# Modulation vectors in the latent attention: two blocks of weight rows at a time, with the eight products ordered behind one another

## The chip, the cores and the metric

The kernel runs on one core of one Trainium2 chip. The metric is device time in microseconds (us) of one execution. Before the change the median of three runs is 1400.68 us (1398.75 to 1402.11).

## The reference, cut to what matters

One encoder layer runs on 1024 prompt frames and 64 sample frames. A conditioning vector c (one per stream, so two) gives six modulation vectors of 1024 elements each, and these shift, scale and gate the layer:

```
mod = silu(c) @ w_ada + b_ada                 # w_ada: 1024 x 6144
shift1, scale1, gate1, shift2, scale2, gate2 = split(mod, 6)
h = rms_norm(x, g_norm1) * (1 + scale1) + shift1
proj = h @ w_in                               # split into latent attention and gated linear attention
x = x + gate1 * (concat(attention, gla) @ w_out)
h2 = rms_norm(x, g_norm2) * (1 + scale2) + shift2
x = x + gate2 * (square(relu(h2 @ w_up)) @ w_down)
```

Vectors 2, 4, 3 and 5 (gate1, scale2, shift2, gate2) are first wanted behind the attention. The change touches how these four are computed.

## The kernel before, in words

Work runs in stages: input projection, gated linear attention, latents and query latents, latent attention (in the trace from about 394 to 605 us), output projection, and the feed-forward layer. Inside a stage several Python generators ("streams") are merged by `interleave` (L50): each `yield pe, wait, cond` says how many nanoseconds of TensorE the piece just written is taken to cost, how long the stream wants to wait before it goes on, and a condition that must hold. `interleave` keeps a planned clock and always goes on with the first stream in its list that is ready. That fixes the order in which instructions are written down. The compiler then orders each engine's instructions itself: an instruction written later may go ahead of one that isn't ready, by the compiler's own estimate. `tc.keep_in_program_order(ins)` takes part of that freedom: it puts `ins` behind the instruction of the same engine that was written just before it. It orders the two, and it neither waits for the first to end nor keeps other instructions from going between.

In the latent attention the streams are, in this order: `weights`, `wo_early`, `mods`, `keys_stream`, `queries_stream`, three `worker`s (one head of one tile of queries each) and `out_early`. `mods` (L1174) computes the four vectors one after the other with `mod_vec` (L148), and takes for each one of the four `mm` banks of PSUM, counted in `state["banks"]`; the workers count theirs in the same place.

`mod_vec` sees the 1024 x 1024 weights of a vector as eight blocks of 128 rows by 1024 columns (512 KB each). A block k is loaded by SP into one of three buffers (`raw`, L155) and multiplied on TensorE by four products (L166). Product j takes the 128x32 operand `scT` as stationary matrix and 256 columns of the block as moving one, and writes partitions 32j to 32j+31 of the accumulator: the four use the four column quarters of the array. The trace holds two records for each product, so eight for a block. Three blocks are loaded ahead, and behind block k's products the load of block k+3 is written, which has to wait for block k's buffer. Behind the eighth block ScalarE copies the accumulator (L174), TensorE transposes it (L178) and VectorE adds the bias (L181).

Three facts of the code set the pace. `wait` begins at 3500 where no rows are handed in (`was is None`), as here. Behind the first block it becomes `min(wait, after)`. Each block adds 500 of planned TensorE time. The planned pace of a vector is so 8 times 4.0 us and 1.8 us around it.

Other callers: `shifts` (L395) calls `mod_vec` for vector 0 during the input projection with `after=1500`. `wo_early` (L1138) goes on when the last queries are projected and `mods` is done.

Of the kernel before, what the change touches and what calls it, by code (L numbers as in the profile page):

```python
# [21 lines left out]
KT = D // P  # L22
# [49 lines left out]
def layer(ctx: ExitStack, tc: tile.TileContext, I, O):  # L72
    nc = tc.nc
    ACT, DVE, POOL, PE, SP = nc.scalar, nc.vector, nc.gpsimd, nc.tensor, nc.sync
# [10 lines left out]
    def tp_bank():  # L85
        return psT.tile([P, 512], F32, name="tp")
# [27 lines left out]
    scT = const.tile([P, KT, 32], F32, name="scT")  # L114
# [30 lines left out]
    def mod_rows(m, k):  # L145
        return I["w_ada"][k * P:(k + 1) * P, m * D:(m + 1) * D]

    def mod_vec(m, wpool, tag, mpool, bank, ahead, was=None, after=3500):  # L148

        wait = 3500 if was is None else 1000  # L150
        was = dict(was or {})

        def load(k):
            was[k] = wpool.tile([P, D], F32, name=tag)
            SP.dma_start(was[k], mod_rows(m, k))  # L155

        for k in range(ahead):
            load(k)
        acc = None
        for k in range(KT):  # L160
            yield 0, wait, None
            wait = min(wait, after)
            if acc is None:
                acc = bank()
            for j in range(4):
                mm = PE.matmul(acc[32 * j:32 * j + 32, 0:256], lhsT=scT[:, k, :], rhs=was[k][:, 256 * j:256 * (j + 1)],  # L166
                               start=(k == 0), stop=(k == KT - 1), tile_position=(0, 32 * j))
                if not ahead:
                    tc.keep_in_program_order(mm)
            if k + ahead < KT and ahead:  # L170
                load(k + ahead)
            yield 500, 0, None
        ms = mpool.tile([P, 256], F32, name="lat", bufs=1)
        ACT.copy(ms, acc[:, 0:256])  # L174
        yield 0, 1000, None
        tp = tp_bank()
        for hf in range(2):
            PE.transpose(tp[:, hf * P:(hf + 1) * P], ms[:, hf * P:(hf + 1) * P], ident)  # L178
        src = tp[:, 0:256].rearrange("p (h j r) -> p j h r", h=2, r=32)[:, :, :, 0:2]
        bia = bT[:, 8 * m:8 * m + 8].rearrange("p (j h s) -> p j h s", h=2, s=1).broadcast_to([P, 4, 2, 2])  # L180
        DVE.tensor_tensor(out=modT[:, m].rearrange("p (j h) s -> p j h s", h=2), in0=src, in1=bia, op=ALU.add)  # L181
        if m in (1, 4):
            i, gT = (0, g1T) if m == 1 else (1, g2T)
            DVE.tensor_scalar(out=G12[:, i], in0=modT[:, m], scalar1=1.0, scalar2=None, op0=ALU.add)
            DVE.tensor_tensor(out=G12[:, i], in0=G12[:, i],
                              in1=gT.rearrange("p (k s) -> p k s", s=1).broadcast_to([P, KT, 2]), op=ALU.mult)
        yield 300, 0, None
# [4 lines left out]
    rawp = wctx.enter_context(tc.tile_pool(reuse_waits="tile", name="rawp", bufs=3, side="right"))  # L192
# [29 lines left out]
    def has(*keys):  # L222
        return lambda: all(k in done or k in groups for k in keys)
# [8 lines left out]
    def attn_pool(name, bufs):  # L232
        return actx.enter_context(tc.tile_pool(reuse_waits="tile", name=name, bufs=bufs))
# [41 lines left out]
    with ExitStack() as sctx:  # L275
# [182 lines left out]
        def shifts():  # L458


            yield 0, 1000, has("half 1 1", "h 1")
            load_x(2)
            yield from mod_vec(0, rawp, "raw", dp, mm_bank, 3, after=1500)
            sh = modT[:, 0]
            split(h["h"][:, :, TOK:], h["l"][:, :, TOK:], sh, DVE)
            done.add("shift")
            for c in range(3):
                c0, cn = CHUNKS[c]
                yield 2000, 0, has(f"qk {c}")
                for k in range(KT):  # L470
                    for s, a, b in spans(c):
                        x, s1 = hf[:, k, a:b], sh[:, k, s:s + 1]
                        if k % 2:
                            DVE.tensor_scalar(out=x, in0=x, scalar1=s1, scalar2=None, op0=ALU.add)
                        else:
                            ACT.activation(h["h"][:, k, a:b], x, AF.Identity, bias=s1)
                            DVE.scalar_tensor_tensor(out=h["l"][:, k, a:b], in0=x, scalar=s1, in1=f32(h["h"][:, k, a:b]),
                                                     op0=ALU.add, op1=ALU.subtract)
                    if k % 2:
                        split(h["h"][:, k, c0:c0 + cn], h["l"][:, k, c0:c0 + cn], hf[:, k, c0:c0 + cn], DVE)  # L480
                    yield 0, 300, None
# [692 lines left out]
    def mods():  # L1174
        for m in (2, 4, 3, 5):
            yield 500, 0, lambda: state["banks"] < 4 and has("UQ")()
            state["banks"] += 1
            yield from mod_vec(m, rawp, "raw", aw, mm_bank, 3)
            state["banks"] -= 1
        done.add("mods")  # L1180

# [47 lines left out]
    aw = attn_pool("aw", 2)  # L1229
    qctx = ExitStack()  # L1230
    qw = qctx.enter_context(tc.tile_pool(reuse_waits="tile", name="qw", bufs=2))
    interleave([weights, wo_early(), mods(), keys_stream(), queries_stream(), worker(), worker(), worker(), out_early()])
    actx.close()

# [147 lines left out]
    def bank():  # L1382
        rr[0] += 1
        return (mm_bank, mm_bank, mm_bank, mm_bank, tp_bank, tp_bank, g_bank, g_bank)[rr[0] % 8]()

    with ExitStack() as uctx:
# [130 lines left out]
        chain, side, acc = {}, {}, {}  # L1517
# [323 lines left out]
```

## Time and profile before

| | before |
|---|---|
| median of three runs | 1400.68 us |
| the profiled execution: its time, and its span in the trace | 1400.09 us, 1398.3 us |
| TensorE busy, mean granted clock | 96% of the span, 0.992 |
| VectorE, ScalarE, GpSimd busy | 64%, 47%, 10% |
| DMA | 135 GB/s over the span |

The profile is one execution. PE is TensorE's matmuls, PEld its weight loads, DVE VectorE, ACT ScalarE, POOL GpSimd, SP the engine that issues most DMAs. An engine that is busy all the time isn't at its peak: matmuls are pipelined, and the end of one lies behind the start of the next. What one instruction takes of TensorE's time is therefore best read as the distance from its start to the start of the next.

### The profile page before, as it was taken

How to read it: one execution, taken by the hardware profiler on the slowest of the kernel's cores; microseconds unless marked ns; L12 is line 12 of the kernel's file. 1: busy time of each engine (PE TensorE's matmuls, PEld its weight loads, DVE VectorE, ACT ScalarE, POOL GpSimd, SP SyncE). 2: the span in 40 equal slices, each digit the busy share in tenths (PEclk: the TensorE clock that was granted, in tenths of full speed). 3: DMA queues.
4: the chain of work that ended last, by engine and by line, in shares of the span. 5: the costliest groups of instructions: out<-in, count | busy, mean ns of one | idle time of the engine just before them, and what ended most of it. 6: DMA issues, size and time to landing. Idle time of an engine off the chain costs nothing.

```text
span 1398.3 us, 26315 instructions
## 1 busy us (share of the span) xinstructions
PE 1340.3 (96%) x10014; PEld 1258.9 (90%) x10014; DVE 899.3 (64%) x2034; ACT 654.3 (47%) x1623; POOL 134.3 (10%) x248
## 2 busy tenths in 40 slices
PE   6998899987999999999998999999999999999998
PEld 5897788886876778899998999999999999999998
DVE  5688787336565765655789766566545866774554
ACT  4465444334335566653475444444444343443342
POOL 0026445112011110000000000000000000000000
PEclk9999999999999999999999999999999999999999
DMA  9320021384243442174224544443348764543440
GB/s 346 116 73 9 16 75 55 107 234 135 86 149 119 159 123 71 40 211 135 75 86 160 167 158 138 137 158 134 111 157 292 278 227 150 188 123 96 127 129 33
DMA packets 165592, 188.15 MB, mean 135 GB/s; under 512 B 16814, under 2 KB 116442, under 8 KB 165466
## 3 DMA queue, kind: packets, MB, share of 16 engines
q1 hardware_dynamic: 158010, 180.90, 40.5%
q10 hardware_dynamic: 7456, 5.57, 1.2%
q8 instruction: 79, 1.29, 0.4%
q14 instruction: 47, 0.39, 0.1%
HBM read 132.97 MB, written 53.46 MB: 133 GB/s over the span
## 4 chain that ended last, share of the span: by engine, by line
PE 81%; DVE 9%; DMA 4%; ACT 3%; POOL 2%; issue 2%; SPq 0%; ACTq 0%; DVEq 0%; POOLq 0%
PE mm L93 14%; PE mm L95 13%; PE mm L94 13%; PE g L93 6%; PE g L95 6%; PE g L94 6%; PE mm L962 3%; PE tp L93 3%; PE tp L95 3%; PE tp L94 3%; PE g L989 3%; PE mm L166 2%; DMA raw<-in_w_in 1%; PE tp L999 1%; DVE ST L723 1%
## 5 line engine op out<-in xcount | busy, mean ns | idle before, releaser
L101 ACT CAST opers<-quad 128x512 fp32r<-128x512 f32 x112 | 69.5, 620 | 185.2 <-PE mm L95 146.6
L102 DVE TENSOR_TENSOR opers<-quad,opers 128x512 fp32r<-128x512 f32 x112 | 77.2, 689 | 114.5 <-ACT opers L101 114.5
L95 PE MATMUL mm<-opers 128*128 128x272 f32 x448 | 129.0, 288 | 0.0
L93 PE MATMUL mm<-opers 128*128 128x272 f32 x448 | 128.6, 287 | 0.3 <-DVE e L1773 0.3
L94 PE MATMUL mm<-opers 128*128 128x272 f32 x448 | 128.3, 286 | 0.0
L93 PE MATMUL mm<-ah,wh 128*128 128x272 f32 x424 | 122.1, 289 | 3.0 <-ACT wh L101 2.4
L94 PE MATMUL mm<-al,wh 128*128 128x272 f32 x424 | 121.6, 288 | 0.0
L95 PE MATMUL mm<-ah,wl 128*128 128x272 f32 x424 | 121.4, 288 | 0.0
L93 PE MATMUL mm<-hh,wh 128*128 128x384 f32 (+2 forms) x264 | 90.7, 347 | 1.7 <-ACT hh L101 1.7
L94 PE MATMUL mm<-hl,wh 128*128 128x384 f32 (+2 forms) x264 | 87.5, 332 | 0.0
L95 PE MATMUL mm<-hh,wl 128*128 128x384 f32 (+2 forms) x264 | 87.3, 331 | 0.0
L93 PEld LDWEIGHTS mm<-opers 128*128 128x128 f32 x448 | 84.6, 189 | 0.5 <-issue 0.5
L95 PEld LDWEIGHTS mm<-opers 128*128 128x128 f32 x448 | 84.4, 188 | 0.0
L94 PEld LDWEIGHTS mm<-opers 128*128 128x128 f32 x448 | 84.1, 188 | 0.0
L93 PEld LDWEIGHTS mm<-ah,wh 128*128 128x128 f32 x424 | 79.9, 188 | 3.8 <-ACT wh L101 2.9
L94 PEld LDWEIGHTS mm<-al,wh 128*128 128x128 f32 x424 | 79.8, 188 | 0.0
L95 PEld LDWEIGHTS mm<-ah,wl 128*128 128x128 f32 x424 | 79.5, 188 | 0.0
L102 DVE TENSOR_TENSOR opers<-ru,opers 128x544 fp32r<-128x544 f32 x108 | 77.5, 719 | 2.2 <-ACT opers L101 2.0
L101 ACT CAST opers<-ru 128x544 fp32r<-128x544 f32 x108 | 69.4, 643 | 13.1 <-PE mm L95 11.7
L101 ACT CAST wh<-ru 128x512 fp32r<-128x512 f32 x67 | 41.3, 618 | 69.7 <-PE g L94 26.1
L102 DVE TENSOR_TENSOR wl<-ru,wh 128x512 fp32r<-128x512 f32 x67 | 45.9, 689 | 36.5 <-ACT wh L101 36.3
L93 PE MATMUL mm<-wh,hh 128*128 128x264 f32 (+3 forms) x216 | 65.2, 303 | 0.7 <-ACT gv L561 0.5
(407 smaller groups left out, 4344.2 us busy)
## 6 DMA issues: line engine op xcount, KB each, us to landing
ru<-u_d SPq DMA_DIRECT2D x108, 272.0 KB, 2.8
raw<-in_w_ada SPq DMA_DIRECT2D x40, 512.0 KB, 4.0
ru<-in_w_up SPq DMA_DIRECT2D x32, 512.0 KB, 4.1
quad<-in_w_down SPq DMA_DIRECT2D x16, 1024.0 KB, 6.7
u_d<-st SPq DMA_DIRECT2D x60, 272.0 KB, 2.1
u_d<-sc SPq DMA_DIRECT2D x45, 272.0 KB, 2.1
raw<-in_w_in SPq DMA_DIRECT2D x22, 256.0 KB, 4.4
x<-in_xo_T SPq DMA_DIRECT2D x8, 544.0 KB, 4.6
```

The lines of the kernel that those rows point to most:

```text
L93: PE.matmul(out, lhsT=ah, rhs=bh, start=first, stop=False, skip_group_check=more)
L94: PE.matmul(out, lhsT=ah, rhs=bl, start=False, stop=False, skip_group_check=more)
L95: PE.matmul(out, lhsT=al, rhs=bh, start=False, stop=last, skip_group_check=more)
L101: ACT.copy(hi, src)
L102: eng.tensor_tensor(out=lo, in0=src, in1=f32(hi), op=ALU.subtract)
L166: mm = PE.matmul(acc[32 * j:32 * j + 32, 0:256], lhsT=scT[:, k, :], rhs=was[k][:, 256 * j:256 * (j + 1)], start=(k == 0), stop=(k == KT - ...
L723: DVE.copy_predicated(ST[:n, :, :n].rearrange("p c (b r h) -> p c b r h", r=2, h=hf)[:, :, :, 1], masks[:n, mlv, :n // 2].rearrange("p (o ...
L962: PE.matmul(sp[:n, :w], lhsT=x[:, hd, :n], rhs=y[:, hd, :w], start=(j == 0), stop=(j == 4))
L989: PE.matmul(op[:n, 0:P], lhsT=pt[:kw, k, :n], rhs=kvs[kt // 4].v[:kw, kt % 4, hd], start=(kt == 0), stop=(kt == nkt - 1))
L999: PE.transpose(tp[:kw, k, :n], pr[k0 // 4][:n, P * k:P * k + kw], ident[:n, :n])
```

## The change

`mod_vec` gets an argument `pair`. With `pair=2` the stream writes the eight products of two blocks in one piece (1000 of planned TensorE time), and every product of the eight but the first is put behind the one before it with `keep_in_program_order`. The two loads that follow (blocks k+3 and k+4) are written behind all eight. `mods` alone calls it so, with `after=5500`; since `wait` begins at 3500, `min(wait, after)` stays 3500. The other caller keeps `pair=1`, and writes what it wrote before.

```diff
-    def mod_vec(m, wpool, tag, mpool, bank, ahead, was=None, after=3500):
+    def mod_vec(m, wpool, tag, mpool, bank, ahead, was=None, after=3500, pair=1):
 
         wait = 3500 if was is None else 1000
...
-        for k in range(KT):
+        for k0 in range(0, KT, pair):
             yield 0, wait, None
             wait = min(wait, after)
             if acc is None:
                 acc = bank()
-            for j in range(4):
-                mm = PE.matmul(acc[32 * j:32 * j + 32, 0:256], lhsT=scT[:, k, :], rhs=was[k][:, 256 * j:256 * (j + 1)],
-                               start=(k == 0), stop=(k == KT - 1), tile_position=(0, 32 * j))
-                if not ahead:
-                    tc.keep_in_program_order(mm)
-            if k + ahead < KT and ahead:
-                load(k + ahead)
-            yield 500, 0, None
+            for k in range(k0, k0 + pair):
+                for j in range(4):
+                    mm = PE.matmul(acc[32 * j:32 * j + 32, 0:256], lhsT=scT[:, k, :], rhs=was[k][:, 256 * j:256 * (j + 1)],
+                                   start=(k == 0), stop=(k == KT - 1), tile_position=(0, 32 * j))
+                    if not ahead or k > k0 or (pair > 1 and j):
+                        tc.keep_in_program_order(mm)
+            for k in range(k0, k0 + pair):
+                if k + ahead < KT and ahead:
+                    load(k + ahead)
+            yield 500 * pair, 0, None
...
-            yield from mod_vec(m, rawp, "raw", aw, mm_bank, 3)
+            yield from mod_vec(m, rawp, "raw", aw, mm_bank, 3, after=5500, pair=2)
```

## Rows read from the trace of the kernel before

**Rows 1.** The page: the span, the busy time of each engine, and the shares of the chain of work that ended last, by engine.

```profile
span 1398.3 us, 26315 instructions
PE 1340.3 (96%) x10014; PEld 1258.9 (90%) x10014; DVE 899.3 (64%) x2034; ACT 654.3 (47%) x1623; POOL 134.3 (10%) x248
...
PE 81%; DVE 9%; DMA 4%; ACT 3%; POOL 2%; issue 2%; SPq 0%; ACTq 0%; DVEq 0%; POOLq 0%
```

**Rows 2.** Busy time of each engine in three stretches of the latent attention, with the granted clock, the DMA engines' share and GB/s: the first and second 81 and 60 us with `mods` in them, and the 65 us behind.

```profile
394.00:475.00 81.00, 78.79 (x539) 54.57 (x538) 53.09 (x162) 42.91 (x163) 11.06 (x17) 0.98 0.50 156
475.00:535.00 60.00, 59.24 (x434) 47.57 (x432) 39.49 (x112) 37.63 (x122) 9.38 (x13) 1.00 0.41 129
535.00:600.00 65.00, 63.37 (x436) 58.06 (x437) 44.26 (x129) 41.96 (x108) 2.66 (x4) 1.00 0.19 53
```

**Rows 3.** What TensorE's matmuls waited for from 475 to 535 us, in the list of waits (us in total, times, longest).

```profile
PE tp L884 <- DVE kn L877: 0.8, 1, 0.8
```

**Rows 4.** The products of line 166 alone in the same two stretches: TensorE's busy time and records, then weight loads, and the sum of both stretches.

```profile
394.00:475.00 81.00, 16.81 (x160) 4.76 (x160) 0.98 0.50 156
475.00:535.00 60.00, 8.28 (x96) 2.03 (x96) 1.00 0.41 129
sum 141.00, PE 25.09 PEld 6.79; mean PE 12.55 PEld 3.40
```

**Rows 5.** TensorE's instructions in order of time around one burst of four products: start, us, engine, line, shapes, records in the row.

```profile
526.20 0.34 PE L94 MATMUL g<-wl,cqh 128*128 128x384 f32 x1
526.37 0.34 PE L95 MATMUL g<-wh,cql 128*128 128x384 f32 x1
526.64 0.64 PE L166 MATMUL mm<-raw,scT 128*32 128x256 f32 x8
527.21 0.44 PE L93 MATMUL g<-wh,cqh 128*128 128x384 f32 x1
527.49 0.34 PE L94 MATMUL g<-wl,cqh 128*128 128x384 f32 x1
527.66 0.34 PE L95 MATMUL g<-wh,cql 128*128 128x384 f32 x1
```

**Rows 6.** The same view: the first burst of the attention (ten records, with the next row behind it), the second (22 records), a block in two parts (two and six records), the sixth and the seventh burst of two records, and the last burst. Between the first and the last there are 35 rows of line 166 in all: 16 of eight records, eight of six, seven of two, two of ten, one of 22 and one of 24.

```profile
394.29 1.05 PE L166 MATMUL mm<-raw,scT 128*32 128x256 f32 x10
395.27 0.49 PE L1195 MATMUL g<-ones,sq 128*128 128x1 f32 x3
...
398.90 1.50 PE L166 MATMUL mm<-raw,scT 128*32 128x256 f32 x22
400.33 0.39 PE L93 MATMUL g<-wh,cqh 128*64 128x384 f32 x1
...
405.94 0.62 PE L166 MATMUL mm<-raw,scT 128*32 128x256 f32 x2
406.49 0.50 PE L93 MATMUL g<-wh,lath 128*128 128x512 f32 x1
...
409.15 0.63 PE L166 MATMUL mm<-raw,scT 128*32 128x256 f32 x6
409.72 0.24 PE L962 MATMUL mm<-khs,qh 128*64 128x64 f32 x1
...
461.03 0.62 PE L166 MATMUL mm<-raw,scT 128*32 128x256 f32 x2
...
475.17 0.62 PE L166 MATMUL mm<-raw,scT 128*32 128x256 f32 x2
...
534.34 0.64 PE L166 MATMUL mm<-raw,scT 128*32 128x256 f32 x8
```

**Rows 7.** The loads of the weight rows (line 155) from 394 to 535 us: how many, and their time from issue to landing (least, median, most); and how long SP stood at such a load until a product had freed its buffer.

```profile
L155 SPq DMA_DIRECT2D raw<-in_w_ada x29: 327/328/763, 395.0 to 522.6; - x29
...
DMA to landing us min/median/max: 3.3/4.0/6.9
...
SPq L155 <- PE mm L166: 71.3, 21, 7.4
```

**Rows 8.** Weight loads on TensorE in a burst of 24 records: the third block's first load waited for its rows.

```profile
470.50 0.59 PEld L166 LDWEIGHTS mm<-raw,scT 128*32 128x32 f32 x16 [0.36 <-issue]
471.27 0.26 PEld L166 LDWEIGHTS mm<-raw,scT 128*32 128x32 f32 x8 [0.17 <-DMA raw<-in_w_ada]
```

**Rows 9.** A fall of the granted clock in the attention, columns as in rows 2, and a burst in it in the view of rows 5.

```profile
437.00:444.20 7.20, 6.05 (x51) 3.94 (x49) 4.62 (x17) 3.56 (x16) 1.33 (x2) 1.00 0.39 111
445.20:448.70 3.50, 3.50 (x15) 2.32 (x15) 2.17 (x6) 2.05 (x7) 0.00 (x0) 0.53 0.06 22
...
445.29 0.99 PE L166 MATMUL mm<-raw,scT 128*32 128x256 f32 x2
446.21 1.12 PE L891 MATMUL tp<-ident,krt 128*128 128x128 f32 x4
```

**Rows 10.** The loads of line 155 from 394 to 475 us.

```profile
L155 SPq DMA_DIRECT2D raw<-in_w_ada x20: 327/328/423, 395.0 to 472.4; - x20
```

## The prediction

> **What bounds the kernel now.** Read the page first: TensorE is busy for 96% of the span, and 81% of the chain that ended last is its own work [rows 1]. An average says little about one stage, so read next the stretches of the attention in which the four vectors are made [rows 2]: TensorE is busy for 78.79 of 81 us and 59.24 of 60 us, VectorE and ScalarE for some two thirds at most, the clock stands at 0.98 and 1.00. In the second stretch TensorE waits for other engines 0.8 us in all [rows 3]. So this stage is bound by TensorE, and time taken from its queue there is mostly time gained. Weight loads fill only 54.57 of the 81 us [rows 2], so TensorE is far from its peak, and something other than data costs it time. The third view shows part of that: the products of line 166, 25.09 us of busy time [rows 4] for vectors that are only multiplied.
>
> **What a burst costs.** Take the distances from start to start around one burst of eight records, that is, one block of weight rows [rows 5]. Between its neighbours a step takes 0.17 us (526.20 to 526.37). The last step ahead of the burst takes 0.27, the burst 0.57 (526.64 to 527.21), the first step behind it 0.28. So the burst costs 0.57 + 0.10 + 0.10 = 0.77 us. How much of it is there once per burst is seen in longer ones [rows 6]: ten records take 0.98 us (394.29 to 395.27), 22 records 1.43 (398.90 to 400.33). Each further pass of the four column quarters adds 0.43; 0.77 - 0.43 = 0.34 is paid per burst. And a quarter alone is no cheaper than four: two records (one product) take 0.55 (405.94 to 406.49), the six others 0.57 (409.15 to 409.72). A block broken into one and three products pays a pass and a burst more, 0.77.
>
> Now count [rows 6]. The 32 blocks stand in 35 bursts; 16 + 8 + 7 of eight, six and two records are one pass each, two of ten are two, those of 22 and 24 three: 41 passes. 41 x 0.43 + 35 x 0.34 = 29.5 us of TensorE's time. Numbered through with eight records to a block, the rows also tell where blocks break: 11 of 32 are broken, each behind its first product.
>
> **The change part by part.**
> *Pairs.* The same 128 products are written as 16 pieces of eight. If each stays whole: 32 passes and 16 bursts, 13.8 + 5.4 = 19.2 us, a gain of 10.3. If every pair breaks between its blocks: 32 and 32, 24.6 us, a gain of 4.9. If every pair breaks behind its first product (one, then seven in two passes): 48 and 32, 31.5 us, a loss of 2.0. Those are the bounds, since no burst of a whole pair is in the trace. The pins order the products and forbid nothing between them, so I don't take the breaks as gone: with half the pairs whole, a quarter broken at one place and a quarter at the other there are 8 + 8 + 8 = 24 bursts and 16 + 12 + 8 = 36 passes, 15.5 + 8.2 = 23.6 us. Value taken: 5.9 us gained. It is nearest to the rate of the rows, a third of the blocks broken, spread over two places.
>
> The row of the burst shows about 0.10 us on each side of a change from the full array to quarters [rows 5]. The Trainium skill (TensorEngine Tiling (Array Packing), Key Properties) says that a change of tiling mode, not of tile, drains TensorE. By that rule alone only bursts count, and 11 fewer would give 3.7 us; by the rows the five passes less give 2.2 more.
>
> *Pace.* `after=5500` changes nothing, because `min(3500, 5500)` is 3500. A vector was planned at 8 x 4.0 + 1.8 = 33.8 us, four at 135; the trace shows 140.6 from the first burst's start to the last one's end (394.29 to 534.34 + 0.57) [rows 6], so the plan holds within 4%. Now it is 4 x 4.5 + 1.8 = 19.8 us, four 79. The vectors will be made by about 476 us instead of 535, nearly twice as fast. Bank: `mods` holds one of four for 79 us instead of 135; I take nothing for it, since heads with two banks of keys come at the sample tile and from the fifth prompt tile on, mostly outside the stretch that is relieved. The copies, transposes and additions behind each vector stay as many; nobody wants them before the attention ends.
>
> *Loads.* Still 32 of 512 KB, on SP. By 475 us, 20 of those in the stretch had been issued before [rows 10]; nine more go into it, 4.7 MB on top of 156 GB/s x 81 us = 12.6 MB, so 214 GB/s and a DMA share near 0.69 where 0.50 was [rows 2]. SP stood at such loads for 71.3 us in all [rows 7], with the loads of query and key latents behind them; those holds get fewer and end sooner, and I take nothing for that either.
> What shrinks is the lead. Before, block k+3 left three blocks ahead of its use, some 12 us by plan. Now the second block of a pair leaves when the pair before has freed the first buffer, and is wanted 0.43 + 3.5 + 0.43 = 4.4 us later; landing takes 3.3 to 6.9 us, 4.0 in the median [rows 7]. There are three such places per vector, 12 in all, and TensorE takes its instructions in order: behind a waiting product stand the products of keys, queries and all three workers. Bounds: 0, where the compiler puts other work ahead, and 12 x (6.9 - 4.4) = 30 us where every load is the slowest. The one row where a burst caught its rows waited 0.17 us [rows 8]; I take 12 x 0.17 = 2.0 us. Below nothing isn't to be had: a wait gives no time back.
>
> **Sum.** -5.9 + 2.0 = -3.9 us: 1396.2 us against the profiled execution's 1400.09, of which 1.8 us lie around its span. The median of the runs is 0.6 above that execution, so I put it at 1396.8 us.
>
> **Rivals.**
> *The pairs break as the blocks did.* If the pins hold nothing together, and three pairs in four break behind a first product, there are 28 bursts and 36 + 8 = 44 passes, 28.4 us: a gain of 1.1, and waits of 2.0 take it: 1401.6 us, and no change that can be seen (a measurement of this kernel tells about 0.2%, 2.8 us, from nothing). For it: six of the seven bursts of two records lie ahead of 465 us [rows 6], in the very stretch to which all the work now moves. Against: a pair is twice as large a piece, so fewer pieces can be broken.
> *Late rows.* With the DMA share at 0.69, let a load land 1.0 us after it is wanted instead of 0.17, which is 5.4 us and within rows 7. 12 places cost 12 us, and a fall of the clock may follow, as it did behind a stretch in which TensorE was busy for 6.05 of 7.2 us: the clock went to 0.53, that is to 1.2 GHz, and a burst of one product took 0.92 instead of 0.55 [rows 9], so with 3.5 us at half speed 1.7 us more. -5.9 + 12 + 1.7 = +7.8: 1408.5 us. It decides from 5.9 / 12 = 0.5 us per place on. Against it: the order of rows 8 shows that a load's landing is estimated about right. The Trainium skill (DMA: Bandwidth & Descriptors, Rules for kernel authors) speaks for it: issue a DMA early, compute, and wait late; the change waits earlier. No row shows yet what a shorter lead costs.
> *Crowded, then starved.* All products now fall before 476 us. Before, 16.81 of 25.09 us of them did [rows 4], by share 19.8 of the 29.5; now 23.6, 3.8 more. Behind, 9.7 us of work go. If the attention there is held by its own chains, none of these come back: 1400.7 + 3.8 = 1404.5. It decides when less than 3.8 of the 9.7 come back. Against: waits of 0.8 us [rows 3], and 63.37 of 65 us busy without the vectors [rows 2].
> *All whole:* -10.3 and no waits, 1390.4 us.
>
> **How the numbers follow.** The forecast 0.38 (its own range 1393 to 1398), all whole or nearly 0.12, pairs broken 0.28, late rows 0.12, crowded 0.10. The first two make faster 0.50, the third same 0.28, the last two slower 0.22. From 1390.5 to 1404.5 the range leaves out half of all whole and most of late rows, some 0.18.
>
> **What would show it.** Rows of line 166 in the profile after: 24 in the attention if I am right, with rows of 16 records near 1.0 us; 35 or more for the broken pairs. The last of them near 476 us; if it is near 535, the pace is misread. Waits of PE or its weight loads at line 166 for `in_w_ada`: about 2 us; over 6 us it is late rows. PE busy from 476 to 535 us above 95%, or else starved. I am wrong altogether if the attention ends as before while line 166 costs 6 us less.

## The result and the profile after

The changed kernel takes 1408.59 us in the median of four runs (1406.95 to 1409.15), the kernel before 1400.87 in the same session: a ratio of 1.0047, 95% interval 1.0033 to 1.0061. It is slower by 7.7 us. The profiled execution took 1408.33 us.

The page after, with the lines that answer to [rows 1]:

```profile
span 1406.3 us, 26319 instructions
PE 1340.5 (95%) x10014; PEld 1261.9 (90%) x10014; DVE 900.9 (64%) x2034; ACT 657.1 (47%) x1623; POOL 136.5 (10%) x248
...
PE 77%; DVE 10%; DMA 5%; ACT 4%; POOL 3%; issue 2%; SPq 0%; ACTq 0%; DVEq 0%; POOLq 0%
```

TensorE is busy as long as before (1340.5 against 1340.3 us), in a span that is 8.0 longer, and its share of the chain falls from 81% to 77%. So TensorE waits more. Where it does is read from the stretches of [rows 2], after:

```profile
394.00:475.00 81.00, 78.31 (x622) 53.35 (x620) 50.86 (x156) 41.42 (x152) 11.89 (x16) 1.00 0.71 232
475.00:535.00 60.00, 53.76 (x326) 47.06 (x325) 38.95 (x103) 36.23 (x118) 8.46 (x12) 0.97 0.12 33
535.00:600.00 65.00, 60.58 (x424) 55.65 (x423) 44.41 (x129) 42.57 (x112) 4.26 (x6) 1.00 0.15 43
```

The stretch into which all the products moved is nearly as full as before (78.31 us against 78.79) and its DMA share is 0.71. Behind it, where no product is left, PE is busy for 53.76 of 60 us where it was 59.24, and for 60.58 of 65 where it was 63.37.

The products themselves, with line numbers one or two higher after the change (166 is 167): their busy time over the whole attention, beside the sum 25.09 of [rows 4], and some of their rows in TensorE's order of time, with the row behind the last.

```profile
390.00:640.00 250.00, 20.20 (x256) 6.87 (x256) 0.99 0.40 122
...
426.45 0.64 PE L167 MATMUL mm<-raw,scT 128*32 128x256 f32 x8 [0.33 <-DMA raw<-in_w_ada]
...
472.27 1.07 PE L167 MATMUL mm<-raw,scT 128*32 128x256 f32 x16
473.27 0.66 PE L893 MATMUL tp<-ident,krt 128*128 128x128 f32 x4
```

The same 256 records are now 23 rows instead of 35, 12 of them with 16 records (a whole pair, 1.00 us from its start to the next). The distances from each row to the next add up to 19.11 us, before to 23.77. Not all of these 4.7 us are the products' own. Without the waits of the rows behind them the sums are 18.7 and 22.8 us, and 0.4 of the 22.8 is the burst that ran at the low clock [rows 9]. So the products got cheaper by 3.7 us (22.4 to 18.7), and are done at 473 us.

One measure serves for all that follows: TensorE's busy time from 390 to 640 us, a window that holds the attention of every version. Before, then after:

```profile
390.00:640.00 250.00, 245.40 (x1750) 203.68 (x1748) 159.05 (x443) 140.14 (x421) 24.35 (x36) 0.99 0.42 129
```
```profile
390.00:640.00 250.00, 236.66 (x1691) 198.59 (x1690) 156.32 (x435) 140.00 (x418) 24.61 (x34) 0.99 0.40 122
```

It stands idle for 4.6 us before and for 13.3 after, 8.7 more. What it waits for, in the list of waits from 390 to 640 us, first before, then after (us in total, times, longest):

```profile
PE tp L999 <- ACT prob L973: 2.5, 3, 1.2
PE tp L884 <- DVE kn L877: 1.6, 2, 0.9
```
```profile
PE tp L1001 <- ACT prob L975: 6.6, 3, 3.0
PE tp L1001 <- DVE ql L940: 1.1, 1, 1.1
PE g L991 <- ACT qsq L913: 0.9, 1, 0.9
...
PE mm L167 <- DMA raw<-in_w_ada: 0.3, 1, 0.3
```

TensorE waits for softmax weights (`prob`), and then for a little of everything: these are the attention's own chains, mostly (10.7 of the 13.3 us) behind the last product. The costliest wait lies near the end. TensorE's row that ends it, with the first row behind; then VectorE's rows ahead of it; then the chain of waits there:

```profile
596.00 0.60 PE L1102 MATMUL tp<-ident,mo 128*128 128x128 f32 x4
599.61 0.87 PE L1001 MATMUL tp<-ident,prob 128*128 128x128 f32 x4 [3.02 <-ACT prob L975]
600.14 0.77 PE L964 MATMUL mm<-kh,qh 128*128 128x512 f32 x1
600.71 0.63 PE L964 MATMUL mm<-kl,qh 128*128 128x512 f32 x1
```
```profile
596.38 1.23 DVE L105 TENSOR_TENSOR wl<-raw,wh 128x1024 fp32r<-128x1024 f32 x1
597.52 0.68 DVE L967 TENSOR_REDUCE sta<-mm 128x1 f32<-128x512 f32 x1
598.24 0.16 DVE L970 TENSOR_TENSOR sta<-sta 128x1 f32<-128x1 f32 x1
598.44 0.16 DVE L971 SCALAR_TENSOR_TENSOR sta<-sta,ssq 128x1 f32<-128x1 f32 x1
```
```profile
596.63 0.60 ACT mt L1104
...
597.66 0.99 ACT wh L1132
598.64 0.05 issue
598.69 0.88 ACT prob L975 x2
```

The scores of that head were written at some 596.2 us. VectorE first did 1.23 us of splitting `w_out` for the output projection and then the maximum of the scores; ScalarE, in its order, copied a finished tile of heads (L1104) and did a cast for the same projection (L1132). Both queues were through within 0.1 us of each other (598.60 and 598.64), and the exponential starts at 598.69. TensorE had nothing else in front. Behind the wait its scores follow each other at 0.43 us (600.71 to 601.14 and so on) instead of 0.23: the granted clock. Three stretches around it (columns as in [rows 2]):

```profile
596.60:599.60 3.00, 0.00 (x0) 0.00 (x0) 2.79 (x5) 2.53 (x5) 0.00 (x0) 1.00 0.91 240
599.60:603.00 3.40, 3.39 (x11) 2.80 (x12) 1.03 (x4) 3.40 (x8) 0.00 (x0) 0.55 0.61 188
603.00:606.00 3.00, 3.00 (x16) 2.46 (x15) 2.34 (x6) 1.41 (x3) 0.00 (x0) 0.95 0.00 0
```

A pause of 3.0 us is followed by 3.4 us near 1.2 GHz. The pause of 2.44 us that ended at 486.48 was followed by the same (0.61 until 490.0). Before, the attention had one such fall [rows 9].

The pause that ended at 486.48 was a wait for `prob` too. Ahead of that softmax VectorE waited for GpSimd and did two pieces of the next keys, and only then the last step of the statistics (`sta`) that the exponential needs:

```profile
484.12 0.69 DVE L879 TENSOR_TENSOR kn<-kn,ssk 128x512 f32<-128x512 f32 x1 [1.09 <-POOL ssk L877]
484.73 0.69 DVE L880 TENSOR_TENSOR krt<-R,ssk 128x512 f32<-128x512 f32 x1
485.33 0.15 DVE L971 SCALAR_TENSOR_TENSOR sta<-sta,ssq 128x1 f32<-128x1 f32 x1
```

The account, from the first row of the sums over `ones, sq` (358.4 us before, 359.6 after) to the last transposes of `mo` (611.3, 620.8): 252.9 us become 261.2. The products give back 3.7 us (22.4 to 18.7 at full clock). TensorE's gaps add 8.8 (4.9 to 13.7) and the clock 1.7 (1.7 to 3.4). The other instructions take 1.5 more, of which 0.9 are six products of the output projection that now stand ahead of the last transposes. Another 1.2 us lie ahead of the attention. There both traces hold the same instructions of TensorE in the same order, up to 396 us, so this is scatter between two executions and not the change. Behind the attention the two differ by little: the feed-forward layer begins 8.7 us later.

### The profile page after: what moved, and what is told of

The parts are those of the page before. It is cut to its first block, busy times and chain, and to the rows that moved or that the text cites. A ratio compares the mean times of both kernels' runs of the same rounds, so it can differ in the third digit from the quotient of the medians.

```text
span 1406.3 us, 26319 instructions
## 1 busy us (share of the span) xinstructions
PE 1340.5 (95%) x10014; PEld 1261.9 (90%) x10014; DVE 900.9 (64%) x2034; ACT 657.1 (47%) x1623; POOL 136.5 (10%) x248
## 4 chain that ended last, share of the span: by engine, by line
PE 77%; DVE 10%; DMA 5%; ACT 4%; POOL 3%; issue 2%; SPq 0%; ACTq 0%; DVEq 0%; POOLq 0%
PE mm L93 14%; PE mm L95 13%; PE mm L94 13%; PE g L95 5%; PE g L93 5%; PE g L94 5%; PE tp L93 3%; PE tp L95 3%; PE tp L94 3%; PE mm L964 3%; PE g L991 2%; DMA raw<-in_w_in 2%; PE mm L167 1%; PE tp L1001 1%; DVE ST L725 1%
```

## The experiments

Two theories stood against each other. *Starved*: the rival of the prediction; the products were filler for waits that the attention has anyway, and now there is none behind 473 us. *Dealt anew*: the waits come from the order that the compiler gives the rest of the attention; it changes with every change of the products' pace, and the order of the kernel before has few waits. A third question was what the pairs are worth apart from the pace. The pins do nothing here: compiled without them, the changed kernel has the same instructions in the same order on all five engines.

Times are medians in us beside the kernel before on the same chip; "plan" is the planned time of a vector, worked out as in the prediction (the first piece of a vector always waits 3.5 us); "products" is their busy time on TensorE in the attention; "idle" is 250 minus PE's busy time from 390 to 640 us, "tail" 70 minus that from 570 to 640. The last three columns are read from one profiled execution, and a run of a few us above or below the median can differ in them: the profiled executions of `e9`, `e14`, `e15` and `e17` lie 2.6 to 4.2 us from their medians, the others less.

| run | plan | time | before | ratio, interval | products | idle | tail |
|---|---|---|---|---|---|---|---|
| before | 33.8 | 1400.87 | | | 25.09 | 4.6 | 1.3 |
| after | 19.8 | 1408.59 | 1400.87 | 1.0047 (1.0033, 1.0061) | 20.20 | 13.3 | 3.0 |
| e1_single_fast | 19.8 | 1411.75 | 1401.70 | 1.0073 (1.0060, 1.0085) | 24.11 | 12.6 | 5.5 |
| e2_pairs_slow | 33.9 | 1410.34 | 1401.70 | 1.0072 (1.0052, 1.0092) | 23.47 | 11.4 | 5.0 |
| e3_pairs_mid | 25.8 | 1403.52 | 1401.70 | 1.0008 (0.9998, 1.0018) | 20.61 | 10.3 | 3.0 |
| e4_fast_two_again | 19.8 | 1417.82 | 1401.70 | 1.0112 (1.0098, 1.0126) | 31.23 | 11.5 | 4.9 |
| e5_single_3300 | 32.4 | 1410.35 | 1401.71 | 1.0062 (1.0045, 1.0080) | 24.11 | 11.5 | 4.8 |
| e6_single_3700 | 35.2 | 1408.61 | 1401.71 | 1.0047 (1.0032, 1.0062) | 26.99 | 7.1 | 2.7 |
| e7_single_3000 | 30.3 | 1411.64 | 1401.71 | 1.0070 (1.0055, 1.0085) | 25.12 | 12.2 | 5.0 |
| e8_single_4000 | 37.3 | 1406.73 | 1401.71 | 1.0036 (1.0024, 1.0048) | 26.97 | 6.4 | 1.4 |
| e9_single_3300_wo | 32.4 | 1409.49 | 1402.10 | 1.0053 (1.0037, 1.0068) | 24.11 | 11.9 | 2.6 |
| e10_after_wo | 19.8 | 1409.05 | 1402.10 | 1.0052 (1.0037, 1.0067) | 20.20 | 12.1 | 1.9 |
| e11_pairs_mid_wo | 25.8 | 1399.64 | 1402.10 | 0.9986 (0.9975, 0.9996) | 20.61 | 6.3 | 0.7 |
| e12_before_wo | 33.8 | 1402.64 | 1402.10 | 1.0008 (0.9998, 1.0018) | 24.79 | 5.9 | 1.8 |
| e13_pairs_4500 | 22.8 | 1409.30 | 1401.57 | 1.0058 (1.0038, 1.0079) | 22.49 | 11.4 | 4.7 |
| e14_pairs_5000 | 24.3 | 1400.77 | 1401.57 | 0.9997 (0.9987, 1.0006) | 21.64 | 5.6 | 1.5 |
| e15_pairs_6200 | 27.9 | 1405.21 | 1401.57 | 1.0029 (1.0013, 1.0045) | 23.27 | 8.9 | 3.0 |
| e16_pairs_7000 | 30.3 | 1409.31 | 1401.57 | 1.0055 (1.0038, 1.0073) | 22.24 | 12.1 | 4.8 |
| e17_pairs_5000_wo | 24.3 | 1401.27 | 1401.39 | 0.9998 (0.9989, 1.0008) | 21.64 | 6.7 | 0.4 |
| e18_pairs_6200_wo | 27.9 | 1402.18 | 1401.39 | 0.9998 (0.9989, 1.0006) | 23.71 | 6.3 | 0.8 |

### Pairs and pace apart

`e1` has the pace of the changed kernel with single blocks, against the changed kernel:

```diff
-            yield from mod_vec(m, rawp, "raw", aw, mm_bank, 3, after=5500, pair=2)
+            yield from mod_vec(m, rawp, "raw", aw, mm_bank, 3, after=1500)
```

> One block at a time as before (pair=1), but with 1.5 us between blocks, so that a vector is planned at 3.5 + 7 x 1.5 + 8 x 0.5 + 1.8 = 19.8 us, the pace of the changed kernel. The built order has 36 bursts and 39 passes in the attention, 29.0 us of TensorE's time, as much as before. Theory 'crowded, then starved' (the pace is the cause): the products are gone by about 476 us, TensorE waits some 9 us more behind them, as in the changed kernel, and nothing is saved: 1407 to 1413 us. Theory 'late rows' (the second block of a pair waits for its load): every block still has three blocks of lead, so no loss: 1399 to 1402 us.

`e2` has the pairs at the pace of before. For this, and in all runs named `pairs`, `after` is made to count; `e2` passes `after=8200`, and `e3` the 5500 that is written:

```diff
-            wait = min(wait, after)
+            wait = after if pair > 1 else min(wait, after)
```

> Pairs and pins as in the changed kernel, but with 8.2 us between pairs in earnest, so that a vector takes 33.9 us by plan as before and the last products stand near 535 us. The built order has 29 bursts and 41 passes, 27.5 us, 2.0 less than before. Starved: the products fill TensorE's waits to the end of the vectors as before, so 1397 to 1401 us, and the time that TensorE waits from 475 to 600 us is back near 2 us. Late rows: the lead is 9 us, no wait at line 167, 1397 to 1401 us too. A third theory, that pairs as such upset the order of the attention, expects 1405 us or more.

> Pairs with 5.5 us between them in earnest, the value that the call names: 25.8 us per vector by plan, the last products near 500 us. The built order has 21 bursts and 37 passes, 23.0 us, 6.5 less than before. Starved: about half of the stretch behind the vectors is uncovered, so some 4 to 5 us of the 9 are lost: 1397 to 1401 us, between the slow and the fast pairs in TensorE's waits behind the vectors. Late rows: the lead is 6.4 us, so hardly a wait, and the whole gain shows: 1393 to 1396 us.

Measured: 1411.75, 1410.34 and 1403.52 us. *Late rows* expected less in all three runs (1402 us at most for `e1`), so rows that land late are not the cause. `e1` lies in the range of *starved*, but `e2` and `e3` lie above it (1401 us at most). For `e2` only the third theory, that pairs as such upset the order, had such a time. By the medians either half of the change alone is slower than both together; for `e2` the intervals overlap. At the fast pace the pairs gain 3.1 us (1411.75 to 1408.59), which agrees with the products: from row to row, without the waits behind them, they take 21.75 us in `e1` and 18.74 after. At the pace of before they lose 8.6, with products that are no dearer (23.47 us busy against 25.09) and 6.8 us more of idle time. So it is not the speed alone that costs.

### More work for the empty stretch

`e4` computes vectors 2 and 4 a second time behind the four, in the changed kernel; nothing is left out.

```diff
-        for m in (2, 4, 3, 5):
+        for m in (2, 4, 3, 5, 2, 4):
```

> The changed kernel, with the first two vectors (2 and 4) computed a second time behind the four, with the same values: 64 more products, some 9 to 10 us of TensorE's time in 14 bursts, and 16 more loads, from about 476 to 516 us. Starved: TensorE has idle time there that these fill, so the time rises by less than half of what they cost: 1409 to 1413 us. If TensorE isn't starved there, they cost all of it: 1417 us or more.

Measured: 1417.82 us, 9.1 more than after by the ratios (0.0065 of 1401.7). Its products over the attention, and the whole window:

```profile
390.00:640.00 250.00, 31.23 (x384) 10.28 (x384) 0.98 0.48 149
```
```profile
390.00:640.00 250.00, 238.54 (x1737) 191.08 (x1736) 150.94 (x428) 137.37 (x416) 24.79 (x34) 0.98 0.48 149
```

Half as many products again (384 records, the last at 516 us) cost 11.0 us of busy time, and the idle time only goes from 13.3 to 11.5 us. If the waits behind 473 us were there for want of filler, this filler would have been nearly free; *starved* expected 1409 to 1413 us. It pays almost its full price. The stretch in which the new products stand, after and in `e4`:

```profile
473.00:516.00 43.00, 38.57 (x231) 33.20 (x224) 28.45 (x80) 26.47 (x92) 6.86 (x10) 0.96 0.16 43
473.00:516.00 43.00, 41.68 (x307) 29.50 (x309) 26.00 (x73) 23.28 (x80) 5.88 (x8) 1.00 0.64 210
```

There TensorE is idle for 1.3 us instead of 4.4, so the new products do fill waits; but the tail waits 4.9 us instead of 3.0. `e1` has the pace of the changed kernel too, with its last products at 483 us, and from 473 to 570 us it is idle for 3.5 us, the changed kernel for 7.6. So want of filler isn't the whole cause, and *starved* falls as the account of the loss. A part of it may be true: with the loads and casts of `w_out` as they are, TensorE is idle from 473 to 570 us for 2.9 to 7.6 us in the versions whose products end by 503 us, and for 1.1 to 4.1 in those where they go on beyond 512.

### Neighbouring paces of single blocks

In the kernel before, `after` is made to count, and passed as 3300, 3700, 3000 and 4000, where the kernel has 3500:

```diff
-            wait = min(wait, after)
+            wait = after
...
-            yield from mod_vec(m, rawp, "raw", aw, mm_bank, 3)
+            yield from mod_vec(m, rawp, "raw", aw, mm_bank, 3, after=3300)
```

> The kernel before, one block at a time, with 3.3 instead of 3.5 us between blocks: the planned pace of a vector goes from 33.8 to 32.4 us, and the products cost the same within 2 us. Theory 'starved' (a fast pace takes the filler away): the last products come 6 us earlier, which is next to nothing: 1400 to 1403 us. Theory 'dealt anew' (any other pace deals the order of the attention's pieces anew, and the order of before has unusually few waits of TensorE, 4.7 us from 358 to 611 us, where the four variants and the changed kernel have 10 to 14): 1404 to 1412 us, with 9 us of waits or more and 3 to 5 of them near 600 us.

> As the run with 3.3, with 3.7 us between blocks, 35.2 us per vector. Starved: 1399 to 1402 us, since the filler lasts a little longer. Dealt anew: 1404 to 1412 us, with 9 us of waits or more.

> As the run with 3.3, with 3.0 us between blocks, 30.3 us per vector. Starved: 1401 to 1404 us. Dealt anew: 1404 to 1412 us, without any order by pace among 3.0, 3.3, 3.7 and 4.0.

> As the run with 3.3, with 4.0 us between blocks, 37.3 us per vector. Starved: 1398 to 1402 us. Dealt anew: 1404 to 1412 us.

Measured: 1410.35, 1408.61, 1411.64 and 1406.73 us. A step of 4% in the plan of a vector (33.8 to 32.4 or 35.2), the same pieces and no pair, costs as much as the whole change did. Their last products stand at 528.6, 540.2, 529.1 and 549.6 us, before at 534.4, so want of filler can't explain them. What they have in common with the changed kernel is idle time on TensorE, 6.4 to 12.2 us; at 3700 and 4000 the products, broken more often, take 1.9 more as well. All four times lie where *dealt anew* expected them (1404 to 1412 us); the waits of 9 us or more that it expected came at 3300 and 3000, and not at 3700 (7.1). The place of the waits changes too: in `e5` the added idle time lies ahead of 473 us (4.2 us, before 2.2) and behind 570 (4.8, before 1.3), in the changed kernel mostly between (7.6, before 1.1). So the question is turned round: 1401 us is the good end of a spread. Whether the kernel before stands there by luck or by earlier tuning is not on record.

Part of that spread has one place. In `e5`, ScalarE and then TensorE near the end:

```profile
593.26 1.04 ACT L1130 CAST wh<-raw 128x1024 fp32r<-128x1024 f32 x1 [2.17 <-DMA raw<-in_w_out]
594.21 0.36 ACT L1014 ACTIVATE mo<-g,sta 128x128 f32<-128x128 f32 x1
595.27 1.04 ACT L1130 CAST wh<-raw 128x1024 fp32r<-128x1024 f32 x1 [0.70 <-DMA raw<-in_w_out]
596.22 0.36 ACT L1014 ACTIVATE mo<-g,sta 128x128 f32<-128x128 f32 x1
```
```profile
596.64 0.57 PE L1100 MATMUL tp<-ident,mo 128*128 128x128 f32 x3 [1.90 <-ACT mo L1014]
599.66 1.11 PE L999 MATMUL tp<-ident,prob 128*128 128x128 f32 x4 [2.46 <-ACT prob L973]
```

ScalarE stands at two casts of `w_out`, whose rows have not landed, for 2.9 us. The scaling of a head's output is behind them in its order, and TensorE waits 1.90 us for that and 2.46 for the next softmax. They are the fourth and fifth of five blocks. The first three were loaded from 523.7 us on, but their casts are written only when `mods` is done and the last queries are projected, and begin at 586.84. The other two loads need the buffers that these free, and are issued at 589.44 and 590.59 us.

### The casts of `w_out` earlier

In four kernels `wo_early` begins when `mods` is done and the keys of tile 7 are, without waiting for the last queries: three blocks of `w_out` are loaded and two cast (in `e9` at 536.2 and 537.8 us, with the next two loads at 538.6 and 540.4). From the third block on its casts wait for the last queries, as before:

```diff
+            if m == 2:
+                yield 0, 0, has("proj end")
...
-        yield 0, 0, has("proj end", "mods")
+        yield 0, 0, has("k 7", "mods")
```

> The kernel with 3.3 us between single blocks, whose end of the attention has two waits of TensorE (1.9 and 2.5 us near 596 and 600 us): there ScalarE stands at two w_out casts for 3.1 us until their rows land, with the scaling of the last head's output and the next exponentials behind them. Here the first two of the five w_out blocks are cast as soon as the keys and the four vectors are done, and the other three when the last queries are projected, as before. Theory 'ScalarE's queue at the end': the casts find their rows landed, the two waits shrink to below 2 us together, and the time falls by 2 to 4 us: 1406 to 1408 us. Theory 'dealt anew and nothing more': the waits stay between 3 and 5 us or come back elsewhere, 1408 to 1413 us.

> The changed kernel with the same earlier casts. Its wait near 600 us (3.0 us) stands behind w_out casts and the subtractions that go with them on VectorE. ScalarE's queue: that wait shrinks below 1.5 us, 1405 to 1407 us. Dealt anew: 1406 to 1412 us with 10 us of waits or more in all.

> Pairs with 5.5 us between them and the earlier casts. ScalarE's queue: the wait of 3.0 us near 595 us shrinks below 1.5, and the time goes below the kernel before: 1398 to 1401 us. Dealt anew: 1402 to 1408 us.

> The kernel before with the earlier casts. It has no wait of TensorE near 600 us, so ScalarE's queue has nothing to give there: 1399 to 1403 us if the rest of the order stays. Dealt anew: 1404 to 1412 us, as in the four runs with another pace.

Measured: 1409.49, 1409.05, 1399.64 and 1402.64 us. `e9` and `e10` miss what the casts were to give (1406 to 1408 and 1405 to 1407 us); `e11` and `e12` came as forecast. The tail of `e9` and `e10` lost 2.2 and 1.1 us of idle time, but the ratios of `e9` and `e5` differ by 0.0009 and those of `e10` and after by 0.0005, less than the intervals are wide: other waits came, in `e9` between 539 and 565 us. At 5500 in pairs the edit took 3.9 us (3.1 by the ratios), and that version is the fastest of all, 0.14% below the kernel before. Its window and its tail:

```profile
390.00:640.00 250.00, 243.68 (x1760) 204.16 (x1760) 160.11 (x445) 142.37 (x422) 25.49 (x36) 1.00 0.42 128
...
570.00:640.00 70.00, 69.26 (x515) 65.41 (x514) 42.90 (x99) 36.91 (x79) 2.82 (x4) 1.00 0.46 133
```

The wait of 3.0 us for `prob` that `e3` has in its tail is gone. The kernel before had no such wait and gains nothing.

### More orders

Pairs at four more paces (`after` of 4500, 5000, 6200 and 7000), and the earlier casts at two of them:

> Pairs with 4.5 us between them in earnest (22.8 us per vector). 26 bursts and 39 passes in the built order, 25.6 us of TensorE's time, 3.9 less than the 29.5 of before. Theory 'dealt anew, pairs gain': the order of the attention is one of many, with waits of TensorE from 390 to 640 us between 6 and 14 us (before: 4.6), and the pairs take 3 to 5 us off what single blocks had in such orders (1406.7 to 1411.8, mean 1409.8 over five): 1402 to 1409 us, mean of the four runs of this call 1405 to 1407. Rival 'pairs gain nothing': as single blocks, mean 1409 to 1411. Rival 'before is only one of many orders': one or more of the four at 1397 or below.

> Pairs with 5.0 us between them (24.3 us per vector), 26 bursts. As the run with 4.5: 1402 to 1409 us; pairs gain nothing: 1407 to 1412 us.

> Pairs with 6.2 us between them (27.9 us per vector), 28 bursts. As the run with 4.5: 1402 to 1409 us; pairs gain nothing: 1407 to 1412 us.

> Pairs with 7.0 us between them (30.3 us per vector), 25 bursts. As the run with 4.5: 1402 to 1409 us; pairs gain nothing: 1407 to 1412 us.

> Pairs with 5.0 us between them, and the earlier w_out casts. The end of the attention without the earlier casts has waits of only 1.4 us from 570 to 640 us, so ScalarE's queue gives 1 us at most: 1399 to 1401 us. Dealt anew: 1401 to 1408 us.

> Pairs with 6.2 us between them, and the earlier w_out casts. Without them the end of the attention has one wait of 3.0 us near 594 us, as with 5.5 us. ScalarE's queue: it shrinks below 1.5 us and the time falls by 2 to 4 us, to 1401 to 1403 us. Dealt anew: 1404 to 1408 us.

Measured: 1409.30, 1400.77, 1405.21 and 1409.31 us without the casts moved (mean 1406.15), 1401.27 and 1402.18 with. The time jumps by 8.5 us for 1.5 us of plan (22.8 to 24.3) and back again: no slope in the pace, as *dealt anew* says. The mean lies in the range that it expected for pairs that gain (1405 to 1407); of the four, which were to lie from 1402 to 1409, `e13` and `e16` are 0.3 above and `e14` is 1.2 below. Of the 11.4 us that `e13` is idle, one wait is 4.6; its row on TensorE:

```profile
593.98 0.79 PE L964 MATMUL mm<-kh,qh 128*128 128x512 f32 x1 [4.61 <-ACT prob L975]
```

The earlier casts came as forecast in `e18` and 0.3 us above it in `e17`. They take 3.0 us off `e15` (4.3 by the ratios), which waits in its tail (3.0 us idle to 0.8), and nothing off `e14`, whose tail was 1.5.

Pairs over seven paces (after, `e2`, `e3`, `e13` to `e16`) take 1406.7 us in the mean; single blocks over five (`e1`, `e5` to `e8`) 1409.8, with the kernel before among them 1408.4. The advantage of the pairs is so 1.7 to 3.1 us, in orders that differ by 10, and not clear of that spread. Like with like, it was measured at three paces: 3.1 us at a plan of 19.8 (`e1` and after; 3.6 by the ratios), 2.3 at 30.3 (`e7` and `e16`; 2.1 by the ratios), and a loss of 8.6 at 33.8 and 33.9 (before and `e2`).

## Why the prediction was wrong

**What a burst costs: right. How the pairs break: right in the sum, by luck.** 24 bursts and 36 passes were forecast; there are 23 and 36, and by the same two prices 15.5 + 7.8 = 23.3 us against the 23.6. But 12 pairs are whole instead of 8, and the other four stand in 11 rows, where eight were to stand in 16; the two misses cancel. The compiler decides that, not the pins. Rows of 16 records take 1.00 us as forecast. Without the two steps beside a burst the prices are 0.43 a pass and 0.14 a burst, which gives 22.5 us before and 18.7 after; measured are 22.4 and 18.7. So 3.7 of the 5.9 us are shown. The other 2.2 are the steps beside 11 bursts, which were not measured after the change.

**Pace: right.** The last burst starts at 472.27 us (476 forecast), and the DMA share of the first stretch is 0.71 (0.69).

**Loads: right in size.** TensorE's weight loads waited 1.1 us in all for the rows, at two places, the longest 0.76, and its products 0.33 at one of them (2.0 forecast, at twelve). *Late rows*, which would have given the very time that was measured, is not what happened.

**Sum: wrong, and this is the step that failed.** It has two terms, the products and their rows, and holds everything else at its old times. A third term was missing: TensorE's waits in the rest of the attention, 4.6 us before and 13.3 after, with 1.7 us of clock behind the longer ones. The prediction read the low waits of [rows 3] as a property of the stage (bound by TensorE, so time taken from its queue is time gained). They are a property of one order of it: `e5` changes nothing but the wait between single blocks, by 0.2 us, and has 11.5 us of idle time. The text on the kernel says that the compiler orders each engine's instructions by its own estimate; that another pace would so give another order got no price.

**Crowded, then starved: the right sign and place, in the main another mechanism.** It gave 1404.5 and "PE busy from 476 to 535 us above 95%, or else starved"; PE was busy for 90% of that stretch. But filler put back there pays nearly its full price (`e4`), single blocks at the same pace wait less than half as long from 473 to 570 us (`e1`), and waits come as well where the vectors end as late as before (`e5` to `e8`). The crowding by itself came: 20.20 us of products in the first stretch where [rows 4] have 16.81.

**Pairs break as the blocks did: wrong,** as the 23 rows show.

**The sum of what is shown:** products -3.7, gaps +8.8, clock +1.7, the other instructions +1.5 and, ahead of the attention, +1.2 of scatter make +9.5 at the end of the attention, of which 8.0 are left in the span.

What stays open: which choice of the compiler makes each order good or bad. One place was shown, the work for the output projection in the queues of ScalarE and VectorE ahead of the last softmaxes; removing it helped in `e11` and `e18`, and in `e9` and `e10` as much came back elsewhere. For the changed kernel itself the cause of each wait is read from its trace, not tried: of the 8.7 us more that it is idle, 6.6 lie from 473 to 570 us, and no run took them away by themselves.

## What to carry to other kernels

Where a planner's times feed a compiler that orders an in-order engine by itself, the pace of one stream is also a throw of dice for all the others: measure the spread first, by moving the pace a few per cent with the work unchanged (here 1401 to 1412 us), and give every forecast a term of that size. A saving of 5 us is then judged over several paces, or like with like at one. A kernel at the good end of such a spread loses by most changes: of the 19 versions here 13 are slower, five can't be told from it and one is faster. Remove the waits that make orders bad (here a cast of late weights ahead of a softmax, which helped in two of the six versions where it was moved) rather than look for the next lucky order.

## What was not expected of the hardware

The prediction knew a fall of the granted clock from one stretch of some 7 us that was less busy [rows 9]. A single short pause can be enough: behind the pauses of 2.44 and 3.02 us in the changed kernel the clock stood at 0.61 and 0.55 for some 3.4 us, and scores came every 0.43 us instead of 0.23; behind the one of 4.61 us in `e13` it stood at 0.50. Where the clock falls, a wait of 3.0 us so costs some 4.5, an estimate from these rows: 3.0 and 0.45 x 3.4 behind it.

But it does not fall each time. In `e15`, TensorE stood just as long at the same place (3.01 us, up to 593.85), and the clock stayed up:

```profile
590.90:593.90 3.00, 0.05 (x1) 0.05 (x1) 2.79 (x5) 2.56 (x5) 0.00 (x0) 1.00 0.86 241
593.90:597.30 3.40, 3.40 (x19) 2.90 (x20) 1.95 (x8) 3.40 (x8) 0.00 (x0) 1.00 0.59 189
```

So the length of a pause alone doesn't tell what it will cost, and equal waits differ by some 1.5 us between versions.
